# A decoder layer on one core: one store moved to ScalarE's DMA queue, one more block sum made by an adding transfer

## The chip, the cores and the metric

The kernel runs on one core of a Trainium2 chip. Its time is the device time in microseconds; the median of 3 runs stands for it. A core has engines that run side by side, each with its own instruction stream: TensorE (matmul, with a part of its own for loading weights), VectorE, ScalarE, GpSimd and SyncE. SyncE, ScalarE and GpSimd can also issue DMA transfers, each into a queue of its own; 16 transfer engines carry them out.

## The reference

One layer for 512 tokens of width 2048, in float32: a combined projection, dilated window attention, a pooling mixer, gates, an output projection, a layer norm, and a feed-forward part with another layer norm. Only the feed-forward part matters here:

```python
x = layer_norm(DEEPNORM_ALPHA * x + mix, ln_mix_g[layer], ln_mix_b[layer])
f = jnp.square(jax.nn.relu(x @ w_ff1[layer])) @ w_ff2[layer]
x = layer_norm(DEEPNORM_ALPHA * x + f, ln_ff_g[layer], ln_ff_b[layer])
```

`w_ff1` is 2048 x 8192 and `w_ff2` 8192 x 2048.

## The kernel before

Every float32 product is made of three matmuls: each operand is split into a high part (ScalarE copies it into a rounded format) and a low part (VectorE subtracts the high part), and high x high, high x low and low x high are added in PSUM. The helper `split` (lines 87 and 88) does this.

The stage that the change touches is the first feed-forward product, FF1. Its 8192 columns are cut into 16 groups of 512. The first is multiplied plainly; the other 15 are units (`FUnit`, g = 1 to 15). A unit splits its weights into four blocks, named 11, 12, 21 and 22 (half of the rows, then half of the columns), and makes seven block products M1 to M7 from sums of blocks in place of eight. Each product is two pieces (`FPiece`, j = 0 to 13, in the order M1, M5, M6, M3, M7, M2, M4): a piece is one half of a block, split into `wh` and `wl` (three buffers each), and 24 matmuls of 256 columns (line 657).

Four sums of blocks are needed. Block 11 is used as loaded for M1, then 12 is added for M5, then 22 for M6; these two sums are made by VectorE (`sum`, line 612), a half block after each split. Block 12 has 22 added for M7 (the third sum); this is one DMA within SBUF with an addition, issued by GpSimd at j = 0 (line 673). Block 11 has 21 added for M4 (the fourth sum); this is made by VectorE in two halves at j = 8 and 9. Pieces 10 and 11 split block 21, pieces 12 and 13 block 11.

The order is written by hand. Before the matmuls of piece j the loop emits the split of piece j + 2 and then `beside(u, j, last)`, where the other work has its place: copies of products out of PSUM, the blocks of the result (line 666), loads of the next unit's weights into blocks that have become free (`give`, loads on SyncE's queue at line 607, at j = 4, 6, 6, 7, 8, 9, 10 and 11), and small pieces of the layer norm's vectors through GpSimd's queue (`y_load`, at j = 7, `y_rows` and `y_rest`).

`beside` also writes out the hidden activations of the unit before it (`last`). These stand in one tile `hpR` with one buffer. At j = 2 and 3 VectorE adds combinations for the second product (line 542), and at j = 5 and 7 `h_parts_out` takes one half each: ScalarE writes the high part into `hpH` (one buffer, tag t10), VectorE subtracts it in `hpR`, and both are stored to DRAM, 896 KB each in rows of 1 KB. The second product, FF2, reads them from there.

Of the kernel before, what the change touches and what calls it, by code (L numbers as in the profile page):

```python
# [13 lines left out]
OP = mybir.AluOpType  # L14
# [54 lines left out]
def decoder_layer(ctx: ExitStack, tc: tile.TileContext, x, xt, positions, w_in, w_pool, pool_scale,  # L69
                  w_branch_attn, w_branch_pool, w_out, ln_mix_g, ln_mix_b, w_ff1, w_ff2,  # L70
                  ln_ff_g, ln_ff_b, consts, vectors, out, h_parts, h_rest, y_norm, y_parts):
    nc = tc.nc
# [13 lines left out]
    def split(dst_h, dst_l, src):  # L86
        nc.scalar.activation(dst_h, src, AF.Copy)  # L87
        nc.vector.tensor_tensor(dst_l, src, dst_h.bitcast(F32), op=OP.subtract)  # L88
# [421 lines left out]
    def y_load(t, n):  # L510
        c = slice(n * 512, (n + 1) * 512)
        nc.gpsimd.dma_start(low["u"][:, 1], y_norm[t, :, c])
        nc.gpsimd.dma_start(low["g"][:, 0], bcast(ln_mix_g, c))
        nc.gpsimd.dma_start(low["g"][:, 1], bcast(ln_mix_b, c))

    def y_rows(t, n):
        c = slice(n * 512, (n + 1) * 512)
        v, g, b = low["u"][:, 1], low["g"][:, 0], low["g"][:, 1]
        stt = nc.vector.scalar_tensor_tensor
        stt(v, v, ALPHA, g, op0=OP.mult, op1=OP.mult)  # L520
        stt(v, b, ALPHA, v, op0=OP.mult, op1=OP.add)
        if t >= 2 and n % 2:
            nc.gpsimd.dma_start(g, y_parts[t - 2, :, c])
            return lambda: y_rest(t, c)
        nc.gpsimd.dma_start(y_parts[t, :, c], v)
# [18 lines left out]
    def h_parts_out(g, j):  # L544
        r = R[g][:, j]
        h = L2["p"].tile([P, 7, 256], F32R, name="hpH", tag="t10")
        split(h, r[:, 1:], r[:, 1:])
        for e, v in enumerate((h.bitcast(F32), r[:, 1:])):
            nc.gpsimd.dma_start(h_parts[g // 2, e, :, :, 2 * (g % 2) + j].rearrange("s p f -> p s f"), v)

    def h_plain_out(g):
        h = L2["p"].tile([P, 2, 4, 256], F32R, name="hpH", tag="t10")
# [6 lines left out]
    def h_out(g):  # L559

        if g >= 14:
            return {2: lambda: h_plain_out(g)}
        return {2: lambda: h_sums(g, slice(0, 2)), 3: lambda: h_sums(g, slice(2, 4)),
                5: lambda: h_parts_out(g, 0), 7: lambda: h_parts_out(g, 1)}
# [94 lines left out]
    def beside(u, j, last):  # L659

        v = {m: p.rearrange("p (n t) -> p n t", n=2) for m, p in u.ps.items()}
        m1, m5, u2 = low["m"][:, 0], low["m"][:, 1], low["u"][:, 0]
        act = nc.scalar.activation

        def block(slot, in0, in1, op):
            nc.vector.tensor_tensor(R[u.g][:, :, slot], in0.rearrange("p (n t) -> p n t", n=2), in1, op=op)

        def relu(a, b):
            act(R[u.g][:, :, a:b], R[u.g][:, :, a:b], AF.Relu)

        if j == 0:
            last.done()
            nc.gpsimd.dma_start(u.b["12"], u.b["22"], accum_op=OP.add)
        elif j == 2:
            act(m1, u.ps["M1"], AF.Copy)
        elif j == 4:
            act(m5, u.ps["M5"], AF.Copy, scale=-1.0)
            u.give(0, 0)
        elif j == 6:
            act(u2, u.ps["M1"], AF.Copy, scale=-1.0)  # L680
            u.give(0, 1)
            u.give(1, 0)
        elif j == 7:
            u.give(1, 1)
            if u.g > 1:
                y_load(*chunks[0])
        elif j == 8:
            u.sum("11", "21", 0)
            u.give(2, 0)
        elif j == 9:  # L690
            u.sum("11", "21", 1)
            u.give(2, 1)
        elif j == 10:
            block(0, m5, v["M1"], OP.subtract)
            u.give(3, 0)
        elif j == 11:
            u.give(3, 1)
            if u.g > 1:
                u.rest = y_rows(*chunks.pop(0))
        elif j == 12:  # L700
            block(1, u2, v["M5"], OP.subtract)
        elif j == 13:
            block(3, m1, v["M2"], OP.add)
            relu(0, 2)
        if j == 3 and last.rest:
            last.rest()
        if j in last.out:
            last.out[j]()
# [98 lines left out]
    def bcast(v, c=slice(0, DM)):  # L807
        return bass.AP(tensor=v.tensor, offset=v.offset + c.start, ap=[[0, P], [1, c.stop - c.start]])
# [121 lines left out]
    p = PS.tile([P, 512], F32, name="mm", bufs=6)  # L930
# [73 lines left out]
    for p in fpieces:  # L1004
        fill(pos[2])
        beside(p.u, p.j, last)
        if p.u is funits[0]:
            if p.j < 2:
                y_add("12", "11", "12", OP.subtract, p.j)
            elif p.j < 4:  # L1010
                y_sum("P4", "12", p.j - 2)
        if p.u in funits[10:14] and p.j == (13 if p.u in funits[10:14:2] else 4):
            y_load(*chunks[0]) if p.j == 13 else y_rows(*chunks.pop(0))
        p.mult()
        pos[2] += 1
        if p.u is funits[-1] and p.j in (3, 5, 7):
            for m in {3: (0, 1), 5: (2, 3), 7: (4, 5)}[p.j]:
                h_load(0, m)
        if p.j == 13:
            last = p.u  # L1020
# [24 lines left out]
    for n in range(2):  # L1045
# [10 lines left out]
        for T in range(2):  # L1056
            v = rows[0, T][:, :, n]
# [52 lines left out]
```

## Time and profile before

| | |
|---|---|
| median of 3 runs | 2421.62 us (2420.31 to 2421.83) |
| profiled execution | 2426.41 us, span 2423.5 us |
| mean granted TensorE clock | 0.996 |
| TensorE busy | 99% of the span |
| VectorE busy | 64% |
| ScalarE busy | 40% |
| GpSimd busy | 8% |

The time of an execution is a little more than its span, which goes from the first to the last instruction. TensorE's busy time is made of pipelined matmuls with modelled ends. FF1 lies between about 1184 and 1789 us of the span. An instruction's idle time is named after what ended it, and a transfer is timed from its issue to its landing.

### The profile page before, as it was taken

To read this page: it belongs to the slowest core of one execution; us is meant where nothing else is said; L and a number is where in the kernel's file an instruction comes from. 1 tells how busy PE (TensorE), PEld (TensorE's weight loads), DVE (VectorE), ACT (ScalarE), POOL (GpSimd) and SP (SyncE) were. 2 spreads that over 40 slices of the span, in tenths; PEclk is the share of its full clock that TensorE was granted. 3 is DMA by queue.
4 is the path that set the end of the run, shared out by engine and by line. 5 is a ranking of instruction groups with operands and counts; after the bars stand their busy time and mean duration, and the time that the engine had idled before them with its cause. 6 is when DMAs were issued, how large, how long until landed. Compare 5 with 4: busy or idle time off the path is not lost.

```text
span 2423.5 us, 31773 instructions
## 1 busy us (share of the span) xinstructions
PE 2394.1 (99%) x13096; PEld 2079.8 (86%) x13096; DVE 1552.7 (64%) x1618; ACT 963.8 (40%) x1033; POOL 182.5 (8%) x271
## 2 busy tenths in 40 slices
PE   9999999999999999999999999999999999999998
PEld 7888888877788888888999999999988888888886
DVE  4532345455533334347877878788867888889886
ACT  4323311244432223127655656555544333333330
POOL 0000000000000000001011111212121000110000
PEclk9999999999999999999999999999999999999999
DMA  6232333322223333346778787878896556665642
GB/s 210 87 96 100 105 96 96 95 79 79 79 87 96 96 96 113 124 155 226 228 220 270 218 274 213 273 231 253 267 371 234 190 175 225 214 237 180 207 164 92
DMA packets 205041, 415.07 MB, mean 171 GB/s; under 512 B 12512, under 2 KB 75104, under 8 KB 202208
## 3 DMA queue, kind: packets, MB, share of 16 engines
q1 hardware_dynamic: 164272, 257.84, 33.0%
q0 software_dynamic: 38320, 151.01, 19.4%
q10 hardware_dynamic: 2304, 4.20, 0.5%
q8 instruction: 102, 1.67, 0.3%
q14 instruction: 43, 0.35, 0.0%
HBM read 329.11 MB, written 68.16 MB: 164 GB/s over the span
## 4 chain that ended last, share of the span: by engine, by line
PE 79%; DMA 8%; issue 7%; DVE 3%; ACT 2%; POOL 1%; POOLq 0%; SPq 0%; DVEq 0%; ACTq 0%
PE mm L147 44%; PE pp L793 22%; PE mm L657 7%; PE pp L838 4%; DMA h_parts<-hpH 3%; DMA w<-in_w_ff 2%; DMA h_parts<-hpR 2%; DVE wl L88 1%; ACT hpH L87 1%; PE sc L351 1%; PE tp L383 1%; DMA wr<-in_w_out 1%; DVE w L612 0%; ACT wh L87 0%; PE tp L375 0%
## 5 line engine op out<-in xcount | busy, mean ns | idle before, releaser
L88 DVE TENSOR_TENSOR wl<-wr,wh 128x1024 fp32r<-128x1024 f32 (+1 forms) x228 | 277.4, 1219 | 566.3 <-ACT wh L87 565.8
L87 ACT ACTIVATE wh<-w 128x1024 fp32r<-128x1024 f32 x406 | 427.3, 1058 | 493.6 <-PE pp L793 301.6
L88 DVE TENSOR_TENSOR wl<-w,wh 128x1024 fp32r<-128x1024 f32 x406 | 494.0, 1221 | 108.2 <-ACT wh L87 108.1
L793 PE MATMUL pp<-wh,hop 128*128 128x512 f32 x1568 | 484.9, 390 | 2.8 <-ACT hpR L617 2.8
L87 ACT ACTIVATE wh<-wr 128x1024 fp32r<-128x1024 f32 (+1 forms) x228 | 240.6, 1055 | 615.6 <-PE mm L147 567.0
L147 PE MATMUL mm<-aH,wh 128*128 128x512 f32 (+1 forms) x1024 | 395.3, 386 | 1.0 <-ACT wh L87 0.9
L147 PE MATMUL mm<-aH,wl 128*128 128x512 f32 (+1 forms) x1024 | 386.0, 377 | 1.3 <-DVE wl L88 1.3
L147 PE MATMUL mm<-aL,wh 128*128 128x512 f32 (+1 forms) x1024 | 385.3, 376 | 0.0
L793 PEld LDWEIGHTS pp<-wh,hop 128*128 128x128 f32 x1568 | 295.7, 189 | 64.7 <-ACT hpR L617 3.0
L793 PE MATMUL pp<-wl,hop 128*128 128x512 f32 x784 | 306.1, 390 | 0.0
L657 PE MATMUL mm<-aH,wl 128*128 128x256 f32 x960 | 273.4, 285 | 7.9 <-DVE wl L88 7.8
L657 PE MATMUL mm<-aH,wh 128*128 128x256 f32 x960 | 272.4, 284 | 0.4 <-ACT wh L87 0.4
L657 PE MATMUL mm<-aL,wh 128*128 128x256 f32 x960 | 272.3, 284 | 0.0
L657 PE MATMUL mm<-ys,wh 128*128 128x256 f32 x1440 | 260.2, 283 | 0.0
L147 PEld LDWEIGHTS mm<-aH,wh 128*128 128x128 f32 x1024 | 193.0, 188 | 39.0 <-ACT wh L87 2.5
L147 PEld LDWEIGHTS mm<-aH,wl 128*128 128x128 f32 x1024 | 192.8, 188 | 37.6 <-DVE wl L88 2.1
L147 PEld LDWEIGHTS mm<-aL,wh 128*128 128x128 f32 x1024 | 193.1, 189 | 37.0 <-issue 1.9
L657 PEld LDWEIGHTS mm<-ys,wh 128*128 128x128 f32 x1440 | 224.5, 192 | 0.0
L657 PE MATMUL mm<-ys,wl 128*128 128x256 f32 x720 | 204.8, 284 | 2.7 <-DVE wl L88 2.5
L657 PEld LDWEIGHTS mm<-aH,wl 128*128 128x128 f32 x960 | 184.9, 193 | 9.8 <-DVE wl L88 9.8
L657 PEld LDWEIGHTS mm<-aH,wh 128*128 128x128 f32 x960 | 185.0, 193 | 0.6 <-ACT wh L87 0.6
L657 PEld LDWEIGHTS mm<-aL,wh 128*128 128x128 f32 x960 | 184.9, 193 | 0.0
(174 smaller groups left out, 3062.7 us busy)
## 6 DMA issues: line engine op xcount, KB each, us to landing
w<-in_w_ff SPq DMA_DIRECT2D x232, 512.0 KB, 8.2
wr<-in_w_in SPq DMA_DIRECT2D x127, 512.0 KB, 3.6
hop<-h_parts POOLq DMA_DIRECT2D x98, 512.0 KB, 7.1
h_parts<-hpH POOLq DMA_DIRECT2D x28, 896.0 KB, 7.8
h_parts<-hpR POOLq DMA_DIRECT2D x28, 896.0 KB, 8.6
wr<-in_w_out SPq DMA_DIRECT2D x40, 512.0 KB, 3.6
wr<-in_w_ff SPq DMA_DIRECT2D x32, 512.0 KB, 3.9
w<-w POOLq DMA_DIRECT2D x15, 1024.0 KB, 7.4
```

The costliest lines, as they stand in the source:

```text
L87: nc.scalar.activation(dst_h, src, AF.Copy)
L88: nc.vector.tensor_tensor(dst_l, src, dst_h.bitcast(F32), op=OP.subtract)
L147: nc.tensor.matmul(o, l, r, start=first and j == 0, stop=last and j == 2)
L351: nc.tensor.matmul(p[:, :n], qT[h][:, qb * P:(qb + 1) * P], kT[h][:, :n], start=True, stop=True)
L383: nc.tensor.matmul(p[:, k * P:], vt["v"][:, k, h * HD:(h + 1) * HD], pT[h][:, k, k * P:], start=k == 0, stop=k == 3)
L657: nc.tensor.matmul(o, l, r, start=first, stop=self.j % 2 == 1 and k == 3 and i == 2, skip_group_check=True)
L793: nc.tensor.matmul(u.ps[:, t], l, r, start=q + j == 0, stop=q == 3 and j == 2)
L838: nc.tensor.matmul(o, l, r, start=first and i == 0, stop=last and i == 2)
```

## The change

The store of the high part `hpH` in `h_parts_out` is issued by ScalarE; the store of `hpR` stays with GpSimd. The fourth sum (11 plus 21) becomes one adding DMA within SBUF, issued by GpSimd at j = 3, as the third sum is at j = 0; the two VectorE sums at j = 8 and j = 9 go. The loads that follow them at these places stay.

```diff
@@ -546,7 +546,8 @@
         h = L2["p"].tile([P, 7, 256], F32R, name="hpH", tag="t10")
         split(h, r[:, 1:], r[:, 1:])
         for e, v in enumerate((h.bitcast(F32), r[:, 1:])):
-            nc.gpsimd.dma_start(h_parts[g // 2, e, :, :, 2 * (g % 2) + j].rearrange("s p f -> p s f"), v)
+            q = nc.gpsimd if e else nc.scalar
+            q.dma_start(h_parts[g // 2, e, :, :, 2 * (g % 2) + j].rearrange("s p f -> p s f"), v)
 
     def h_plain_out(g):
@@ -684,11 +685,11 @@
             u.give(1, 1)
             if u.g > 1:
                 y_load(*chunks[0])
+        elif j == 3:
+            nc.gpsimd.dma_start(u.b["11"], u.b["21"], accum_op=OP.add)
         elif j == 8:
-            u.sum("11", "21", 0)
             u.give(2, 0)
         elif j == 9:
-            u.sum("11", "21", 1)
             u.give(2, 1)
         elif j == 10:
             block(0, m5, v["M1"], OP.subtract)
```

## Rows read from the trace of the kernel before

**Rows 1.** The page: busy us, share of the span and instructions.
```profile
PE 2394.1 (99%) x13096; PEld 2079.8 (86%) x13096; DVE 1552.7 (64%) x1618; ACT 963.8 (40%) x1033; POOL 182.5 (8%) x271
```

**Rows 2.** Stretches: start:end, us, busy of PE, PEld, DVE, ACT, POOL; PEclk; DMA share, GB/s.
```profile
1472.00:1499.00 27.00, 25.97 (x217) 25.77 (x216) 21.24 (x20) 12.94 (x13) 6.18 (x9) 1.00 0.99 324
1472.00:1513.00 41.00, 39.97 (x334) 39.77 (x333) 33.25 (x32) 22.56 (x23) 7.07 (x9) 1.00 0.81 246
1184.00:1789.00 605.00, 592.55 (x4894) 589.63 (x4894) 481.84 (x454) 335.41 (x334) 114.89 (x154) 1.00 0.82 254
```

**Rows 3.** Waits in FF1: who for whom, us in total, times, longest us.
```profile
ACT hpH L87 <- DMA h_parts<-hpH: 45.3, 14, 5.4
...
DVE hpR L666 <- DMA h_parts<-hpR: 17.3, 11, 3.5
...
PE mm L657 <- DVE wl L88: 9.1, 11, 1.7
```

**Rows 4.** Timeline of ScalarE, three units: start, us, instruction, idle before.
```profile
1470.27 1.69 ACT L87 ACTIVATE hpH<-hpR 128x1792 fp32r<-128x1792 f32 x1
...
1480.11 1.70 ACT L87 ACTIVATE hpH<-hpR 128x1792 fp32r<-128x1792 f32 x1 [3.98 <-DMA h_parts<-hpH]
...
1511.87 1.68 ACT L87 ACTIVATE hpH<-hpR 128x1792 fp32r<-128x1792 f32 x1
...
1519.90 1.70 ACT L87 ACTIVATE hpH<-hpR 128x1792 fp32r<-128x1792 f32 x1 [2.18 <-DMA h_parts<-hpH]
...
1637.38 1.69 ACT L87 ACTIVATE hpH<-hpR 128x1792 fp32r<-128x1792 f32 x1
...
1647.57 1.70 ACT L87 ACTIVATE hpH<-hpR 128x1792 fp32r<-128x1792 f32 x1 [4.33 <-DMA h_parts<-hpH]
```

**Rows 5.** Timeline of VectorE at 1481 and 1507.
```profile
1481.84 2.03 DVE L88 TENSOR_TENSOR hpR<-hpR,hpH 128x1792 f32<-128x1792 f32 x1 [4.45 <-ACT hpH L87]
1483.78 1.22 DVE L88 TENSOR_TENSOR wl<-w,wh 128x1024 fp32r<-128x1024 f32 x1
...
1507.75 1.22 DVE L88 TENSOR_TENSOR wl<-w,wh 128x1024 fp32r<-128x1024 f32 x1
```

**Rows 6.** Timeline of TensorE: two matmuls with a wait.
```profile
1485.06 0.39 PE L657 MATMUL mm<-aH,wl 128*128 128x256 f32 x1 [1.03 <-DVE wl L88]
...
1652.51 0.39 PE L657 MATMUL mm<-aH,wl 128*128 128x256 f32 x1 [1.38 <-DVE wl L88]
```

**Rows 7.** Timeline of GpSimd from 1499.
```profile
1498.99 0.90 POOL L673 DMA_DIRECT2D w<-w  x1 [5.52 <-DVE w L612]
1513.85 1.00 POOL L549 DMA_DIRECT2D h_parts<-hpH  x1 [13.96 <-ACT hpH L87]
1515.91 0.99 POOL L549 DMA_DIRECT2D h_parts<-hpR  x1 [1.06 <-DVE hpR L88]
```

**Rows 8.** Group of VectorE's block sums; a DMA issue on ScalarE's queue (timeline).
```profile
L612 DVE TENSOR_TENSOR w<-w,w 128x1024 f32<-128x1024 f32 x90 | 110.1, 1223 | 2.1
...
1064.15 0.33 ACTq L979 DMA_DIRECT2D acc<-in_x  x1
```

**Rows 9.** DMA issues: at 1511.3, at 1516 to 1520, all: KB each, us to landing.
```profile
w<-in_w_ff SPq DMA_DIRECT2D x1, 512.0 KB, 3.5
...
w<-in_w_ff SPq DMA_DIRECT2D x2, 512.0 KB, 13.9
...
h_parts<-hpH POOLq DMA_DIRECT2D x28, 896.0 KB, 7.8
```

**Rows 10.** Queues (packets, MB, share): 1494.6 to 1496.6, 1500.4 to 1505.2, 1519.5 to 1523.5.
```profile
q1 hardware_dynamic: 718, 0.71, 106.5%
...
q0 software_dynamic: 128, 1.05, 107.5%
...
q0 software_dynamic: 277, 1.03, 79.1%
q1 hardware_dynamic: 256, 0.26, 20.1%
```

## The prediction

> **What bounds the kernel now.** I read the page first: TensorE is busy 99% of the span [rows 1], so a change elsewhere can only win TensorE's idle time or make more of it. Both edits work in the first feed-forward product (FF1, 1184 to 1789 us), so the table of stretches came next [rows 2]. There TensorE is busy 592.55 of 605 us with 4894 matmuls, 0.121 us each, so a piece of 24 matmuls takes 2.9 us and a unit of 14 pieces 40.7 us. The idle time, 12.4 us, is all that can be won. VectorE is busy 482 us there, ScalarE 335: neither is a bound. The 16 transfer engines are at 0.82 over the stage, but at 0.99 for 27 us of a unit [rows 2]. Transfers are what is scarce.
>
> The waits of FF1 name what ends the idle time [rows 3]: TensorE waits 9.1 us for `wl` parts of weight pieces. Behind these stand two transfers: ScalarE waits 45.3 us (14 times) until a store of `hpH` has landed, because `hpH` has one buffer and the second half's `hpH` is written over the first's; VectorE waits 17.3 us for a store of `hpR`.
>
> The first wait decides. In the unit at 1470 the first `hpH` activation starts at 1470.27, the second, after 3.98 us of idling, at 1480.11 [rows 4]. The subtraction of `hpR` (1481.84) and only then `wl` of piece 10 (1483.78) follow on VectorE [rows 5], and TensorE starts on that `wl` after idling 1.03 us [rows 6]. Starts 9.84 us apart: 1.03 us lost. At 1637 they are 10.19 apart and 1.38 is lost; at 1511 they are 8.03 apart [rows 4, 6], and I found no wait of TensorE there. The loss is the distance less 8.8 us, with no slack beyond that.
>
> **Part 1, the queue of the `hpH` store.** 28 stores (14 units, two halves) go from GpSimd's queue to ScalarE's. Removed: GpSimd's issue, 0.98 us, and the descriptors made there; the next work on GpSimd waits for VectorE anyhow (1.06 us before the `hpR` store at 1515.91 [rows 7]), so nothing is won by that. Added on ScalarE: one issue, 0.33 us by the only row of its queue [rows 8], behind the activation that it waits for. What is queued behind it is `wh` of the next piece; `wl` of that piece comes after a 2.03 us subtraction [rows 5], which covers 0.33 us. What matters is how soon the store lands. Distance = 1.70 (activation) + landing + 0.1, so the break-even of 8.8 is a landing 7.0 us after the activation. Now the median is 7.8 from issue [rows 9].
>
> A hardware queue sends these 1 KB rows one to a packet: alone, 718 packets at 47.5 ns (106.5% of 16 engines in 2 us) [rows 10]. GpSimd's queue sends packets of 4 KB: from 1519.5 to 1523.5 it had 277 packets and 1.03 MB, the hardware queue 256 packets and 0.26 MB [rows 10]. That is 183 ns a packet (0.791 x 64 us / 277) and one packet each in turn: beside GpSimd's queue, a hardware queue gets a fifth of the bytes. What this does to a transfer is seen in SP's 512 KB loads: 3.5 us to land alone, 13.9 us for two issued while `hpH` and `hpR` were under way [rows 9]. The bounds for 896 KB: alone 3.5 + 24 more packets per engine x 0.0475 = 4.6 us; like those loads 13.9 x 1.75 = 24 us.
>
> The Trainium skill ("DMA: Bandwidth & Descriptors", section "Queues, rings and completion order") says that each engine serves the queues in turn, a packet at a time; the packet counts above agree. By its typical packet of 9 to 17 descriptors a 1 KB row would not be a packet of its own, which the rows contradict; with such packets the store would hold its share of the bytes and land in about today's 7.8 us, and the sum would be near zero.
>
> **Part 2, the adding transfer.** Removed: 30 sums on VectorE, 1.22 us each [rows 8], 37 us of an engine that is no bound. Two sums stood after `wl` of pieces 10 and 11; they can shorten later waits, not the one above, since `wl` of piece 10 comes before them. Added: 15 adding transfers of 1 MB, issued at piece 3. GpSimd waits there for `wl` of piece 5 (1507.75 + 1.22 = 1508.97 [rows 5]), then issues in 0.90 us [rows 7]. Behind it are, in some units, a 256 KB store of `y_parts` and else the `hpR` store, 7 us later: GpSimd idles 13.96 us there today [rows 7], so the wait itself costs nothing. Its result is read by the split of piece 12, over 15 us later; the load of block 21 that it needs was issued six pieces earlier, 17 us, more than the 13.9 of a slow load. Both nothing.
>
> Its load on the engines is not nothing. The 128 packets of 8 KB took 107.5% of 16 engines for 4.8 us, 645 ns each, 5.2 us per unit [rows 10]. From 1472 to 1513 the engines are busy 0.81 of 41 us, 33.2; with 5.2 it is 38.4 of 41 (an `hpH` store itself costs each engine 56 x 47.5 ns = 2.7 us in small packets, 14 x 183 ns = 2.6 in large ones). It just fits, but the place is bad: issued at 1509.0, and with 1.5 us of lead (my estimate), it holds the engines from 1510.5 to 1515.7, while `hpH` (activated 1511.87 to 1513.55 [rows 4]) is to leave from 1514.6.
>
> **The sum.** `hpH` needs 56 packets on each engine, so 56 turns. About 3 turns stand beside packets of the adding transfer (0.74 us each: 2.2). SP's first two loads of the unit, 64 packets per engine and now held back by the same transfer, share the next turns (0.096 each). 14 turns stand beside `hpR`, whose packets come, as I take it, 2 to 3 us after its issue at 1515.9 (0.23 each: 3.2), and 4 beside the `y_norm` vector that follows it on GpSimd's queue (0.9). 35 turns are left, 3.4. In all 9.7 us, and with the lead and tail of a transfer (3.5 less 32 x 0.0475: 2.0) a landing of 11.7 us. I take 12, since other vectors follow. Each unit then loses 12 - 7.0 = 5.0 us: 14 x 5.0 = 70. Gone are today's 9.1 us of TensorE's waits: those for `hpH` are in the 70, and those behind `hpR` go, because `hpR` no longer stands behind `hpH` in one queue. Net +61 us. The profiled execution took 2426.41 us, 4.8 above the median of 2421.62; +61 on either gives 2487 for a profiled one and 2483 for the median. The bounds: at 4.6 us nothing is lost and 9 to 12 are won (2410); at 24 us 14 x 17 - 9 = +229.
>
> **The rivals.** *Hidden, and a gain.* The store leaves 1 us after ScalarE's issue and shares the engines better than I count; landings stay under 7.3 us (14 x 0.3 less 9.1 is -4.9), and up to 12 us of TensorE's idle time goes: 2410 to 2417. For it: the lead on GpSimd's queue is longer (a median landing of 7.8 for 14 packets of 183 ns, 2.6 us). Against: adding transfer, SP's loads and `hpH` need 2.1 + up to 3.0 + 2.7 us from 1513.6 on, which ends by 1520.9 only if the lead is short and `hpR` waits. It decides at a landing of 7.3 us. The Trainium skill (same page, section "Specifications") gives a hardware queue 0.6 us to the first byte against 1 us, which speaks for this rival; no row here shows the first byte. Chance 0.18.
>
> *No change.* Landings of 7.3 to 8.0 us, about today's: what is lost behind `hpH` is what the vanished waits give back, within 5 us of 2421.6. Chance 0.13. The same would come if only bytes counted on shared engines. The Trainium skill (same page, section "Issuing engines are not separate DMA queues") says a second issuing engine saves only issue time; by that rule part 1 is worth nothing, and the time would be that of this rival. The 3.5 and 13.9 us of equal loads speak against it.
>
> *A smaller loss.* The engines overlap an adding packet with others, or ScalarE's queue gets more turns: landing of 8.0 to 9.7 us, 1.0 to 2.7 us per unit less the 9, 2427 to 2450. Chance 0.19.
>
> *A larger loss.* Units with the `y_parts` store, and the slow vector packets after `y_norm`, push the landing to 15 to 18 us: 14 x 8 to 11 less 9, 2524 to 2566. Chance 0.10. Else my forecast, 2450 to 2524: chance 0.40.
>
> **How the numbers follow.** Measuring this kernel tells apart about 0.2%, 4.8 us. Faster 0.18, same 0.13, slower 0.69. The time is that of the forecast, 2483 us; its own range is 2450 to 2524. The range of all runs from 2411, almost the whole of the gain, to 2545, half of the larger loss, and leaves out at most 1 in 10.
>
> **What would show it.** Right: `hpH` stores from ScalarE landing 10 us and more after issue; ScalarE's waits for them at 100 us rather than 45; TensorE's waits for `wl` once per unit, 3 to 7 us, after the second `hpH`; the distance less 8.8 again equal to the loss; waits for `hpR` gone; the stage some 60 us longer. Wrong: landings under 7 us, which would sink the argument by packets in turn; or short landings and a longer stage all the same, through late weight blocks, which I price at nothing.

## The result and the profile after

The changed kernel takes 2532.93 us (median of 4 runs, 2529.91 to 2534.15) against 2421.72 us of the kernel before in the same session: ratio 1.0458, interval 1.0445 to 1.0471. It is slower by 111 us. The profiled execution took 2533.89 us, its span is 2531.8 us against 2423.5, 108.3 more. Line numbers after `h_parts_out` are one higher than before (the matmuls of FF1 are L658, those of FF2 L794).

The page's row of TensorE, for [rows 1]: the same 13096 matmuls now make 96% of a longer span.

```profile
PE 2426.5 (96%) x13096; PEld 2108.4 (83%) x13096; DVE 1521.5 (60%) x1588; ACT 964.5 (38%) x1033; POOL 168.2 (7%) x258
```

The waits of the changed kernel from 1184 to 1900 us, for [rows 3] (who for whom, us in total, times, longest):

```profile
ACT hpH L87 <- DMA h_parts<-hpH: 124.3, 14, 12.2
...
PE mm L658 <- ACT wh L87: 63.3, 14, 7.8
...
PE mm L658 <- DVE wl L88: 13.6, 15, 1.1
DVE low L520 <- DMA low<-in_ln_mix_g: 12.0, 1, 12.0
...
PE pp L794 <- ACT hpR L618: 10.7, 1, 10.7
...
POOL hop L720 <- DMA w<-w: 6.3, 1, 6.3
```

Three more lines of the same view of the kernel before (1184 to 1790 us):

```profile
DVE low L520 <- DMA low<-in_ln_mix_g: 3.8, 1, 3.8
...
PE pp L793 <- ACT hpR L617: 2.8, 1, 2.8
...
PE mm L657 <- ACT wh L87: 0.4, 1, 0.4
```

ScalarE's wait for the store of `hpH` has grown from 45.3 to 124.3 us, still 14 times, once per unit. TensorE now waits in all 14 units, first for `wh` (63.3 us) and right after it for `wl` (13.6); before it was 9.1 us for `wl` and 0.4 for `wh`. VectorE's wait for a store of `hpR`, 17.3 us in [rows 3], no longer appears. The wait of 10.7 us stands where FF1 passes into FF2; it was 2.8 before. Behind it VectorE waits 12.0 us, 3.8 before, until a vector of the layer norm has been loaded. That load itself takes 14.9 us against 13.9, but GpSimd issues it later: a `hop` load ahead of it in GpSimd's order waits 6.3 us until the last unit's adding transfer has landed.

The chain of work that ended last says the same in order of time (start, us, what):

```profile
1425.91 13.87 DMA h_parts<-hpH
1444.81 27.49 PE mm L658 x213
1475.00 14.59 DMA h_parts<-hpH
1494.62 28.09 PE mm L658 x213
1525.41 14.32 DMA h_parts<-hpH
```

From 1184 on one store of `hpH` and one run of matmuls take turns, 14 times: the store is on the path that sets the end.

In one unit ScalarE's timeline shows it, for [rows 4 and 8] (start, us, instruction, idle before):

```profile
1473.29 1.68 ACT L87 ACTIVATE hpH<-hpR 128x1792 fp32r<-128x1792 f32 x1
1475.00 0.37 ACTq L550 DMA_DIRECT2D h_parts<-hpH  x1
...
1478.09 1.06 ACT L87 ACTIVATE wh<-w 128x1024 fp32r<-128x1024 f32 x1 [1.05 <-PE mm L658]
1489.67 1.70 ACT L87 ACTIVATE hpH<-hpR 128x1792 fp32r<-128x1792 f32 x1 [10.53 <-DMA h_parts<-hpH]
...
1491.87 1.06 ACT L87 ACTIVATE wh<-w 128x1024 fp32r<-128x1024 f32 x1 [0.50 <-ACT hpH L87]
```

The two activations start 16.38 us apart, 7.6 more than the 8.8 at which nothing is lost. TensorE's timeline, for [rows 6], shows 6.17 + 0.84 us of idling behind it, and something else after it:

```profile
1492.97 0.58 PE L658 MATMUL mm<-aH,wh 128*128 128x256 f32 x1 [6.17 <-ACT wh L87]
...
1494.62 0.58 PE L658 MATMUL mm<-aH,wl 128*128 128x256 f32 x1 [0.84 <-DVE wl L88]
1494.99 0.41 PE L658 MATMUL mm<-aH,wh 128*128 128x256 f32 x1
...
1500.10 0.28 PE L658 MATMUL mm<-aL,wh 128*128 128x256 f32 x1
```

A matmul lasts 0.41 us until 1499.7 and 0.28 from there on. The table of stretches, for [rows 2], gives the granted clock (the columns are those of [rows 2], PEclk the third from the right):

```profile
1184.00:1892.00 708.00, 626.34 (x4908) 619.40 (x4906) 447.61 (x419) 335.78 (x332) 99.06 (x139) 0.93 0.82 238
...
1486.00:1493.00 7.00, 0.83 (x8) 0.63 (x6) 1.60 (x1) 2.83 (x3) 0.00 (x0) 0.75 0.80 214
1493.00:1499.50 6.50, 5.66 (x25) 5.36 (x26) 4.43 (x5) 1.82 (x3) 0.99 (x1) 0.50 0.97 304
1499.70:1506.00 6.30, 6.30 (x54) 6.30 (x54) 4.82 (x5) 2.47 (x3) 0.58 (x1) 0.99 0.94 309
```

The clock fell during the stall (0.75 on average from 1486 to 1493). After it, it is at 0.50, its lower level of 1.2 GHz, and TensorE does 25 matmuls in 5.66 us of busy time where it then does 54 in 6.30. Over FF1 its busy time is 626.34 us against 592.55.

So the 108 us are, by the rows: idle time in FF1 63.3 + 13.6 - 9.5 = 67.4; at the passage to FF2 10.7 - 2.8 = 7.9; busy time 626.3 - 592.6 = 33.8 (of which 14 more matmul records are 1.7, a shift of the stretch's end). Together 109.1, or 107.4 without the 1.7. From the first matmul of FF1's units to the first of FF2, a stretch with 5042 matmul records in both traces, it takes 732.2 us against 625.0: 107.2 more, of which 32.2 are busy time.

The transfers, for [rows 9] (KB each, median us to landing):

```profile
w<-w POOLq DMA_DIRECT2D x30, 1024.0 KB, 8.2
h_parts<-hpH ACTq DMA_DIRECT2D x28, 896.0 KB, 10.9
```

The median for `hpH`, over both halves, has gone from 7.8 to 10.9; for the 14 first halves alone, the ones that are waited for, the mean is 12.9. Where the time goes is seen in the queues' packets, for [rows 10], in four stretches of the unit above (1472 to 1476, 1476.5 to 1479.5, 1479.5 to 1482.5, 1483 to 1489; q0 is GpSimd's queue, q1 SyncE's, q10 ScalarE's; packets, MB, share):

```profile
q0 software_dynamic: 95, 0.78, 126.8%
...
q1 hardware_dynamic: 850, 0.85, 82.4%
...
q10 hardware_dynamic: 865, 0.88, 82.6%
q1 hardware_dynamic: 206, 0.19, 20.2%
...
q0 software_dynamic: 359, 1.30, 72.8%
q1 hardware_dynamic: 355, 0.36, 21.2%
q10 hardware_dynamic: 20, 0.02, 0.9%
```

In the first stretch, while the adding transfer runs, its packets are the only ones, though SyncE issued loads at 1471.84 and 1474.67 and ScalarE the store at 1475.00. In 13 of the 14 units no packet of SyncE's or ScalarE's queue begins until the last 0.5 us of the adding transfer's packets; in the unit at 1573, 381 packets of SyncE's queue begin among them. (The share is over 100% because a packet's whole time counts where it begins and these packets overlap: they take 0.85 us each, 1.268 x 64 us / 95, against 0.645 us in [rows 10]. What slowed them the records do not say.) In the second stretch SyncE's two loads go, and none of `hpH`. In the third stretch `hpH` goes, 865 of its 896 rows in 3 us. In the fourth 20 packets of it are left, and they take 6 us beside the store of `hpR`, the `y_norm` vectors and the next load. The landing of 14.6 us is some 4.5 of standing behind others, 3 of transfer and 7 of remainder. The remainder belongs to one of sixteen shares of the store. Beside its 896 rows the store has 16 packets of 4 bytes, which I read as the ends of these shares; 15 of them have begun by 1483.3, the last begins at 1489.2. From 1483.4 to 1486.0 the rows still to go follow one another every 0.24 us, which is the turn of 0.23 us that the prediction worked out for a small packet beside a 4 KB one.

### The profile page after: what moved, and what is told of

Same layout as the page of the kernel before. It is cut to its first block, busy times and chain, and to the rows that moved or that the text cites. A ratio compares the mean times of both kernels' runs of the same rounds, so it can differ in the third digit from the quotient of the medians.

```text
span 2531.8 us, 31789 instructions
## 1 busy us (share of the span) xinstructions
PE 2426.5 (96%) x13096; PEld 2108.4 (83%) x13096; DVE 1521.5 (60%) x1588; ACT 964.5 (38%) x1033; POOL 168.2 (7%) x258
## 3 DMA queue, kind: packets, MB, share of 16 engines
q10 hardware_dynamic: 27840, 29.89, 3.4%
## 4 chain that ended last, share of the span: by engine, by line
PE 84%; DMA 9%; ACT 3%; issue 2%; DVE 2%; POOL 0%; DVEq 0%; POOLq 0%; SPq 0%; ACTq 0%
PE mm L147 42%; PE pp L794 21%; PE mm L658 15%; DMA h_parts<-hpH 7%; PE pp L839 3%; ACT hpH L87 2%; DVE wl L88 1%; DMA hop<-h_parts 1%; PE sc L351 1%; PE tp L383 1%; DMA low<-in_ln_mix_b 1%; DMA wr<-in_w_out 0%; PE tp L375 0%; ACT wh L87 0%; PE tp L277 0%
## 5 line engine op out<-in xcount | busy, mean ns | idle before, releaser
L794 PE MATMUL pp<-wh,hop 128*128 128x512 f32 x1568 | 484.6, 390 | 10.7 <-ACT hpR L618 10.7
L794 PEld LDWEIGHTS pp<-wh,hop 128*128 128x128 f32 x1568 | 295.4, 188 | 72.5 <-ACT hpR L618 10.9
L658 PE MATMUL mm<-aH,wh 128*128 128x256 f32 x960 | 287.4, 299 | 63.3 <-ACT wh L87 63.3
L794 PE MATMUL pp<-wl,hop 128*128 128x512 f32 x784 | 305.9, 390 | 0.0
L658 PE MATMUL mm<-aH,wl 128*128 128x256 f32 x960 | 286.7, 299 | 13.3 <-DVE wl L88 13.3
L658 PE MATMUL mm<-aL,wh 128*128 128x256 f32 x960 | 284.7, 297 | 0.0
L658 PE MATMUL mm<-ys,wh 128*128 128x256 f32 x1440 | 260.0, 283 | 0.0
L658 PEld LDWEIGHTS mm<-aH,wh 128*128 128x128 f32 x960 | 198.6, 207 | 66.2 <-ACT wh L87 66.2
L147 PEld LDWEIGHTS mm<-aH,wh 128*128 128x128 f32 x1024 | 193.3, 189 | 39.7 <-ACT wh L87 2.9
L658 PEld LDWEIGHTS mm<-ys,wh 128*128 128x128 f32 x1440 | 224.6, 192 | 0.0
L147 PEld LDWEIGHTS mm<-aH,wl 128*128 128x128 f32 x1024 | 193.1, 189 | 37.7 <-DVE wl L88 2.3
L147 PEld LDWEIGHTS mm<-aL,wh 128*128 128x128 f32 x1024 | 193.2, 189 | 37.1 <-issue 1.9
L658 PEld LDWEIGHTS mm<-aH,wl 128*128 128x128 f32 x960 | 197.7, 206 | 16.9 <-DVE wl L88 16.9
L658 PE MATMUL mm<-ys,wl 128*128 128x256 f32 x720 | 204.3, 284 | 1.6 <-DVE wl L88 1.6
L658 PEld LDWEIGHTS mm<-aL,wh 128*128 128x128 f32 x960 | 198.6, 207 | 0.0
## 6 DMA issues: line engine op xcount, KB each, us to landing
h_parts<-hpH ACTq DMA_DIRECT2D x28, 896.0 KB, 10.9
```

Source lines behind the costliest of these rows:

```text
L147: nc.tensor.matmul(o, l, r, start=first and j == 0, stop=last and j == 2)
L658: nc.tensor.matmul(o, l, r, start=first, stop=self.j % 2 == 1 and k == 3 and i == 2, skip_group_check=True)
L794: nc.tensor.matmul(u.ps[:, t], l, r, start=q + j == 0, stop=q == 3 and j == 2)
```

## The experiments

**Each part alone.** `e1_queue` is the kernel before with the store moved and the VectorE sums kept; `e2_adding` is the kernel before with the adding transfer and the store left on GpSimd's queue.

```diff
# e1_queue, against the changed kernel
-        elif j == 3:
-            nc.gpsimd.dma_start(u.b["11"], u.b["21"], accum_op=OP.add)
         elif j == 8:
+            u.sum("11", "21", 0)
...
+            u.sum("11", "21", 1)
# e2_adding, against the changed kernel
-            q = nc.gpsimd if e else nc.scalar
-            q.dma_start(h_parts[...], v)
+            nc.gpsimd.dma_start(h_parts[...], v)
```

> Part 1 alone: the hpH store goes to ScalarE's queue, the fourth sum stays with VectorE. Theory (packets in turn, with the adding transfer in the way): without the adding transfer the store has only SP's small packets beside it until hpR comes, lands in 7 to 9 us, and the two hpH activations start 9 to 11 us apart: 2415 to 2440 us. Rival A (small packets alone lose against GpSimd's queue): landings stay near the 10.9 us of the changed kernel, over 2480 us. Rival B (the adding transfer alone makes the loss): within 5 us of 2421.7.

> Part 2 alone: the fourth sum is an adding transfer at j = 3, the hpH store stays on GpSimd's queue. Theory: hpH stands behind the adding transfer in the same queue and has 4 KB packets; its descriptors take as long as the rest of the adding transfer, so it lands 0 to 2 us later than before (8 to 9.5 us): 2420 to 2445 us. Rival B (the adding transfer alone, by filling the engines): over 2480 us, with SP's loads and hpR late as well. Rival A: within 5 us of 2421.7.

`e1_queue`: 2415.13 us, ratio 0.9982 (0.9971 to 0.9992), a small gain; `e9_queue_again`, the same kernel once more, 2414.18 us, 0.9975 (0.9965 to 0.9984). The waits of `e1_queue` in FF1:

```profile
ACT hpH L87 <- DMA h_parts<-hpH: 37.2, 14, 4.0
...
PE pp L794 <- ACT hpR L618: 3.4, 1, 3.4
...
PE mm L658 <- DVE wl L88: 2.9, 5, 1.0
```

The unit that corresponds to the one above (timeline of ScalarE):

```profile
1465.93 1.68 ACT L87 ACTIVATE hpH<-hpR 128x1792 fp32r<-128x1792 f32 x1
1467.64 0.37 ACTq L550 DMA_DIRECT2D h_parts<-hpH  x1
...
1474.15 1.70 ACT L87 ACTIVATE hpH<-hpR 128x1792 fp32r<-128x1792 f32 x1 [2.37 <-DMA h_parts<-hpH]
```

And that store in the view of DMA issues (KB, us to landing):

```profile
h_parts<-hpH ACTq DMA_DIRECT2D x1, 896.0 KB, 6.4
```

A store on ScalarE's queue lands 6.4 us after its issue here, under the 7.0 that the prediction gave as break-even. The activations are 8.0 to 9.8 us apart, in 11 of 14 units under 9, where I had expected 9 to 11. So part 1 by itself does what the rival *hidden, and a gain* said of both parts. The gain is small because only 12 us could be won: TensorE's waits in FF1 fall from 9.5 to 2.9 us.

`e2_adding`: 2472.66 us, ratio 1.0219 (1.0202 to 1.0236): more than the 2420 to 2445 us that I expected, and less than the 2480 of rival B. Waits of FF1:

```profile
ACT hpH L87 <- DMA h_parts<-hpH: 75.4, 14, 7.4
...
PE mm L657 <- DVE wl L88: 21.7, 15, 1.8
...
PE pp L793 <- ACT hpR L617: 11.2, 1, 11.2
...
PE mm L657 <- ACT wh L87: 10.1, 7, 2.5
```

The adding transfer hurts a store on GpSimd's queue as well. Part 1 alone is worth -4 to -6 us, part 2 alone +53 (2472.66 less 2472.66 / 1.0219), both +111: together they cost some 63 us more than the sum of each.

**Rows of 7 KB.** `e4_long_rows` lays `h_parts` out so that the stores of `hpH` and `hpR` write 7 KB per row (the queue of ScalarE then has 6336 packets in place of 27840); the `hop` loads of FF2 read 1 KB rows for it. `e6_queue_long` is the same without the adding transfer.

```diff
-            q.dma_start(h_parts[g // 2, e, :, :, 2 * (g % 2) + j].rearrange("s p f -> p s f"), v)
+            q.dma_start(h_parts[g // 2, e, 2 * (g % 2) + j], v)
...
-            nc.gpsimd.dma_start(v[:, e], h_parts[c, e, MO[m][1] - 1])
+            nc.gpsimd.dma_start(v[:, e], h_parts[c, e, :, :, MO[m][1] - 1].rearrange("q p f -> p q f"))
```

> Both parts, and h_parts laid out so that a partition's seven rows of 1 KB are one row of 7 KB (the hop loads of FF2 then read rows of 1 KB instead of 4 KB). Theory: the store needs 8 turns per engine in place of 56, some 0.33 us each, and lands in 6 to 8 us although the adding transfer is there: 2415 to 2435 us, and TensorE keeps its full clock. Rival (bytes or capacity of the engines count, not turns): landings of 10 us and more, 2510 to 2535 us.

> Part 1 alone with the 7 KB rows. Theory: the store lands in 4.5 to 6 us, before the break-even of 7.0, so that the waits of ScalarE for hpH go: 2411 to 2418 us, below both kernels. Rival A, if rows' length does not matter: the same time as part 1 alone with 1 KB rows.

`e4_long_rows`: 2481.15 us, 1.0248 (1.0228 to 1.0268). `e6_queue_long`: 2427.04 us, 1.0029 (1.0017 to 1.0041). Both are outside what I had given them, and outside the rivals too. The waits of `e4_long_rows`:

```profile
ACT hpH L87 <- DMA h_parts<-hpH: 74.1, 14, 7.4
...
ACT hpR L670 <- DMA hop<-h_parts: 22.4, 1, 22.4
...
PE pp L794 <- ACT hpR L618: 22.3, 1, 22.3
...
PE mm L658 <- DVE wl L88: 16.0, 15, 1.2
...
PE mm L658 <- ACT wh L87: 13.3, 13, 3.0
```

Inside FF1 TensorE idles 29.3 us in place of 76.9, as much as in `e2_adding` (31.8). So of the 77 us about 47 go with the rows of 1 KB. What they change is the remainder of the fourth stretch above: the first packet of a store still begins 3.8 to 5.1 us after its issue (3.9 to 5.2 in the changed kernel), but it lands after 9.3 us on average in place of 12.9. That it is `hpH`'s rows and not `hpR`'s is not separated, since the edit lengthens both. The other 30 us stay. The whole time shows less of it, because the `hop` loads became slow in exchange (22.3 us at the passage to FF2, 15.5 in `e6_queue_long`); I had not expected that price.

**Later stores.** `e3_late` writes the two halves at j = 7 and 9 in place of 5 and 7, out of the way of the adding transfer; `e8_queue_late` is its control without the adding transfer.

```diff
-                5: lambda: h_parts_out(g, 0), 7: lambda: h_parts_out(g, 1)}
+                7: lambda: h_parts_out(g, 0), 9: lambda: h_parts_out(g, 1)}
```

> Both parts, and the two halves written out two pieces later (j = 7 and 9 in place of 5 and 7), so that the adding transfer is through before the first hpH store leaves. Theory (the store meets the adding transfer): landings of the first hpH store fall back towards those of part 1 alone (about 8 us), ScalarE's wait for it from 124 us to 30 to 50 us; the hpR store has 5.8 us less until the next unit's block wants its place, so a new wait of VectorE appears; 2430 to 2465 us in all, and its control (e8_queue_late) 0 to 25 us less. Rival (the engines are simply full with the adding transfer): landings stay over 10.5 us, 2510 to 2535 us.

> Control: part 1 alone with the halves written out at j = 7 and 9. Theory: the hpH stores land as in part 1 alone; only the shorter time for the hpR store costs: 2418 to 2440 us.

Both missed, and `e3_late` is slower than its rival's range as well. `e3_late`: 2540.77 us, 1.0496 (1.048 to 1.0512); `e8_queue_late`: 2470.62 us, 1.0213 (1.0199 to 1.0227). The waits of `e3_late`:

```profile
ACT hpH L87 <- DMA h_parts<-hpH: 123.9, 14, 10.9
...
PE mm L658 <- DVE hpR L667: 95.5, 14, 8.9
```

TensorE now waits for another instruction (L667, the block of the result that is written late; 43.4 us in the control), so the place costs by itself: 50 us in the control, where 8 of the 14 first stores land after 6.2 to 7.6 us and 6 after 10.2 to 14.6. The adding transfer costs another 70, though it no longer meets the store: in 13 of 14 units of `e3_late` it has landed 2.7 to 3.8 us before the store is issued, and the store still takes 10.1 to 15.0 us. In the packets it stands behind SyncE's loads, which came late: in the unit at 1488 the next 3.8 us have 1082 packets of SyncE's queue and none of ScalarE's. So it is not the store alone that must keep clear of the adding transfer. The pair doesn't separate this from the vector loads of GpSimd, which leave right behind the adding transfer here (1477.31).

**How much of the transfer.** `e7_half` makes only the first half of the fourth sum by the transfer, and the second by VectorE at j = 9.

```diff
-            nc.gpsimd.dma_start(u.b["11"], u.b["21"], accum_op=OP.add)
+            nc.gpsimd.dma_start(u.b["11"][:, :4], u.b["21"][:, :4], accum_op=OP.add)
...
+            u.sum("11", "21", 1)
```

> Both parts, but the adding transfer makes only the first half of the fourth sum (0.5 MB); VectorE makes the second at j = 9 as before. Theory (meeting): 2.6 us of engine time from 1.5 us after the issue end about when the hpH store leaves, so most of the loss goes, not half: landings near 8 us, 2415 to 2440 us. Rival (load of the engines, in proportion): half of the loss stays, 2465 to 2485 us.

`e7_half`: 2419.54 us, 0.9998 (0.9989 to 1.0007). Half of the transfer leaves not half of the loss but almost none (2.1 us of waits in FF1, ScalarE's wait for `hpH` 36.8). In the unit shown above it is over before 1466, and SyncE's first load is issued at 1466.12 and `hpH` at 1467.84. That fits two accounts: the transfer must not meet the loads and the store, or the transfer engines have no room for the second half. The last pair separates them.

**The same bytes, earlier.** `e10_two_halves` makes the whole fourth sum by two transfers of half a block, at j = 2 and 3, each as soon as its half of block 11 is split. `e11_two_halves_pool` does so with the store on GpSimd's queue.

```diff
         elif j == 2:
             act(m1, u.ps["M1"], AF.Copy)
+            nc.gpsimd.dma_start(u.b["11"][:, :4], u.b["21"][:, :4], accum_op=OP.add)
...
-            nc.gpsimd.dma_start(u.b["11"], u.b["21"], accum_op=OP.add)
+            nc.gpsimd.dma_start(u.b["11"][:, 4:], u.b["21"][:, 4:], accum_op=OP.add)
```

> Both parts of the change, with the whole fourth sum still made by GpSimd's queue, but as two transfers of 512 KB, half a block each: the first at j = 2, as soon as that half of block 11 has been split, the second at j = 3. The same bytes are added per unit as in the changed kernel; the first half follows the third sum on GpSimd's queue directly, so both should be through about 2.5 us earlier, before the unit's first hpH activation and before the first of SyncE's loads is due. If the loss comes from the adding transfer meeting these and holding them (my theory now): distances between the hpH activations back at 8 to 9.8 us in nearly all units, ScalarE's wait for hpH under 50 us, no low clock, 2412 to 2435 us. If the loss comes from the bytes themselves (the transfer engines have no room for 5.2 us more per unit; rival): distances stay above 11 us, ScalarE's wait above 90 us and the time above 2480 us. Between 2435 and 2480: both have a part.

> The same two half transfers, with the hpH stores left on GpSimd's queue as in the kernel before (the second part of the change alone, moved earlier). The second part alone, as one transfer at j = 3, took 2472.66 us. By the theory that it is the meeting that costs: within 10 us of the kernel before, about 2420, ScalarE's wait for hpH 40 to 55 us. By the rival of bytes: still above 2455 us.

`e10_two_halves`: 2436.24 us, 1.0074 (1.0061 to 1.0086). `e11_two_halves_pool`: 2439.26 us, 1.0087 (1.0072 to 1.0103). The waits of `e10_two_halves`:

```profile
ACT hpH L87 <- DMA h_parts<-hpH: 52.9, 14, 10.5
...
PE pp L795 <- ACT hpR L618: 9.8, 1, 9.8
PE mm L658 <- ACT wh L87: 8.1, 3, 6.2
...
PE mm L658 <- DVE wl L88: 6.6, 9, 1.1
```

With the same bytes added, the time is 97 us below the changed kernel's. The rival of bytes falls for all but a small part: over 605 us of this kernel's FF1 the transfer engines are at a share of 0.93, above the 0.82 of the changed kernel, so there is no general want of room. The numbers are just outside what I gave them (2412 to 2435 us, under 50 us of waiting, no low clock), in the strip for "both have a part": one unit still has its activations 16.4 us apart and loses 6.2 + 0.8 us, two lose about 2, and the passage to FF2 costs 9.8. In `e11_two_halves_pool` the earlier place takes away 33 us of 53, and 11.7 us are left at the passage. That one is outside its 10 us too.

The pair changes a second thing: the halves go out in packets of 4 KB, not 8. The units of `e10_two_halves` speak for the place. In 11 of them the second half has landed at most 0.7 us after the store's issue, and the store takes 6.2 to 9.5 us. In the unit at 1634 it lands 3.9 us after it, and the store takes 14.6 us, as in the changed kernel, with the smaller packets. In the other two it lands 1.8 and 2.4 us after, and the store takes 6.8 and 9.3. A part of the packets' size in the gain is not excluded.

The best version is `e1_queue`: part 1 of the change, without part 2.

## Why the prediction was right, and what its size left out

The direction, the path (a late store of `hpH` holds TensorE up once per unit) and the range (2411 to 2545 us) held; the time is 50 us above the forecast of 2483, outside the forecast's own 2450 to 2524, and lies in the rival *a larger loss*, with its 0.10. That rival asked for landings of 15 to 18 us; the mean is 12.9, and what carries the time there is another thing, TensorE's clock. So it is partly luck that the range, which took in half of that rival, held.

**The break-even: right; its chain nearly.** The 14 distances between the `hpH` activations add up to 205.4 us. Less 14 x 8.8 that is 82 us; TensorE idled 76.9. The distance still gives the loss, unit by unit (11.42 apart: 1.2 + 1.1 lost; 16.38: 6.2 + 0.8). The prediction had TensorE waiting for `wl`; most of the wait, 63.3 of 76.9 us, is for `wh`, which follows the second `hpH` on ScalarE (1489.67, then `wh` at 1491.87, then the matmul at 1492.97).

**The landing: right in size, in part by luck.** I took 12 us; the mean distance of 14.7 less 1.8 is 12.9. The terms behind the 12 came out differently, as the next paragraph says. The term "14 x 5.0 = 70" came out as 76.9, and today's waits to be taken off as 9.5 in place of 9.1. `hpR` behaved as foreseen: VectorE's waits for its store are gone.

**What makes the landing: half right.** That the rows of 1 KB cost is shown by `e4_long_rows`: with 7 KB rows 47 of the 77 us of idling go. The step "about 3 turns stand beside packets of the adding transfer (0.74 us each: 2.2)" failed: the records show no turns there. From 1472 to 1476 no packet of another queue began, and the store's first packet came 4.6 us after its issue. Nor do SyncE's loads and the store share turns as I counted them: nearly all of the loads went first, and then the store. The Trainium skill ("DMA: Bandwidth & Descriptors", section "Queues, rings and completion order") has each engine go round the queues packet by packet; the rows every 0.24 us of the fourth stretch above agree, the 95 packets of the first stretch do not. The Trainium skill's rule (same page, section "Issuing engines are not separate DMA queues") that another issuing engine only saves issue time would make part 1 worth nothing. Part 1 alone measured 0.18 and 0.25% faster, and with the adding transfer the two issuers are 60 us apart (2472.66 and 2532.93). So in these runs the issuer counts; with it the store's packets change from 4 KB to 1 KB.

**Part 2's cost on the engines: right in kind, wrong in account.** "It just fits, but the place is bad" is what `e10_two_halves` shows: both parts with the same bytes in two halves at a better place cost 17 us and not 111. Wrong is how the sum laid the loss: of the 12 us of landing it gave 2.2 to the adding transfer and most to the queue of part 1. Alone, part 2 costs 53 us and part 1 gains. And what the prediction counted behind the adding transfer on GpSimd leaves out the last unit: there a `hop` load waits for it, and TensorE's wait at the passage into FF2 is 7.9 us longer. The same wait of a `hop` load for `w<-w` stands in `e2_adding` (6.7 us), `e10_two_halves` (4.3) and `e11_two_halves_pool` (3.1), and in `e1_queue` there is none.

**The mis-sized term: TensorE's clock.** The sum priced the time in which TensorE stands, and none for the time after. With each of the 14 stalls the granted clock went to 0.5 for 3.4 to 10.2 us. In 12 units it fell before the stall's last wait was over, in two 0.2 and 0.4 us after. TensorE was busy for some 70 us of these stretches; at the upper level the same matmuls take half of that, so 35 us are the clock's, less 1.7 for the one such stretch that the kernel before has. That is the 32 to 34 us of busy time which the sum lacks. With the 7.9 us at the passage into FF2, which I had priced at nothing, it makes up the difference: 61 + 7 (idle time in FF1) + 8 + 32 is 108. The term could have been seen: the stretch of the kernel before, 3.4 us from 1569.9 on, stands behind a wait of 1.75 us.

**Left open.** Why one share of the store falls so far behind the other fifteen is not shown, and the records do not name the transfer engine. Why distances differ so from unit to unit (11.4 to 18.1) is shown in part: in the four units where GpSimd issues the `y_parts` store 0.6 us behind the adding transfer, `hpH` lands after 13.9 to 16.3 us, in the other ten after 9.6 to 15.4. That much of the rival *a larger loss* is there. A second buffer for `hpH`, which would take ScalarE's wait away, was not tried.

## What to carry to other kernels

An adding transfer frees a compute engine only at the price of the transfer engines: look in the packets at what is to leave while it runs, and put it where nothing is due; here the same bytes cost 17 us in two early halves and 111 us in one later transfer. What the adding transfer holds back counts too: in `e3_late` the store left after it and still stood behind the loads that came late. Where one buffer makes an engine wait for a store, find the latest landing that costs nothing, and count each unit's distance against it. When a forecast contains stalls of TensorE, add the slower matmuls that come with them.

## What was unexpected of the hardware

- While an adding transfer of 1 MB within SBUF ran (8 KB packets), the records show no packet of SyncE's or ScalarE's queue for 4 us, with three transfers issued: 95 packets of GpSimd's queue from 1472 to 1476, and no others; one unit of 14 is an exception. In `e10_two_halves` too, a load issued at 1466.23 had its first packets at 1468.5 to 1469, when the adding packets ended.
- Loads of SyncE's queue and stores of ScalarE's were served mostly in the order of their issue: 850 packets of SyncE's queue and none of ScalarE's in 3 us, then 865 of ScalarE's and 206 of SyncE's.
- A store lands with the last of its 16 shares. In the unit above 15 shares had ended 8.2 us after the issue, the last 14.2 us after it.
- The granted clock fell from 1.0 to 0.5 in or right after stalls of 1.2 to 7.9 us (each with a second wait of 0.8 to 1.1 us behind it) and stayed there for 3.4 to 10.2 us. The length of one stall does not settle it: in the kernel before one of 1.75 us was followed by it and one of 1.38 us was not ([rows 6]; the clock is 1.00 from 1652.9 to 1660), and in `e11_two_halves_pool` two of six stalls of 1.56 to 1.75 us were.
